# The output gate of a gated recurrence: four projection jobs become two pairs of seven block products

## The chip, the core and the metric

The kernel runs on one core of a Trainium2 chip. Its engines run side by side and wait for each other through semaphores: TensorE (PE in the profile, with its weight loads as PEld) multiplies matrices into PSUM; VectorE (DVE), ScalarE (ACT) and GpSimd (POOL) work on elements; SyncE (SP), ScalarE and GpSimd issue the transfers between memory and SBUF. The metric is the device time of one execution in microseconds (us), lower is better.

## What is computed

One hybrid residual block on 1024 tokens of width 1024, in float32. Two branches read the same normalised input; a sigmoid gate for each merges them; an MLP follows. The part around the change, cut from the reference:

```python
u = xn @ w_in[layer]
q_sb, k_sb, v_sb, f_raw, i_hg, q_hg, g_hg, gate_sb, gate_hg = jnp.split(u, list(c), axis=-1)
o_sb = merge_heads(stick_breaking_attention(...))
f = lb + (1.0 - lb) * jax.nn.sigmoid(f_raw)
o_hg = hgrn2_chunkwise(silu(q_hg), (1.0 - lb) * sigmoid(-f_raw), i_hg, log(f))
o_hg = merge_heads(rmsnorm(o_hg, hg_norm_g)) * jax.nn.silu(g_hg)
g_a = jax.nn.sigmoid(gate_sb + bg[:D_MODEL])
g_b = jax.nn.sigmoid(gate_hg + bg[D_MODEL:])
merged = g_a * (o_sb @ w_o_sb) + g_b * (o_hg @ w_o_hg)
h = x + merged @ w_out
```

`g_hg`, the output gate of the recurrent branch, has four heads of 128 columns. `gate_sb` and `gate_hg`, the branch gates, have 1024 columns each.

## The kernel before

**How a product is made.** Every float32 operand is split into a high part (a cast to fp32r, on ScalarE) and a low part (the difference, on VectorE); `hi_lo` issues both. A product of two such operands takes three matmuls (`three`): high by high, high by low, low by high. One matmul is 128 x 128 weights by 512 tokens, so a projection of the 1024 tokens to 128 columns takes 8 chunks x 2 token halves x 3 = 48 matmuls.

**Two streams on TensorE.** The matmuls of the attention and of the recurrence are the "main" lane. Between them the program sets steps of a stream of other jobs, `st` ("fill"), mostly six matmuls a step. The job order is the order of `st.add`. `st.advance(n, upto)` lets the stream run n steps but not past job `upto`; `st.finish(upto)` runs all up to it. When a job starts, `Stream.prefetch` splits the weights of the next one and loads those of the one after it. TensorE's instruction order is thus written out in program order.

**Stages.** Attention; then the recurrence, head by head: `hg_levels(h)` (decay products on VectorE, scores on TensorE, named sl, at seven levels) side by side with `hg_tail(h - 1)` (state sums pkv, outputs pho, norm, transposes pot). At each step of either, `FILL[h]` steps of the stream are added. Then the gate stage `gates()`, then the output projection and the MLP.

**Block products.** The branch gates are made as products of 2 x 2 blocks in seven multiplications in place of eight: two token halves and two input halves by two column blocks, gate_sb's and gate_hg's columns of one block `cb`. For each of eight `cb`, `raw_job(cb)` runs three plain products in the recurrence: bank pga takes two, pgq the third (on a weight sum, `split_t`), 36 matmuls. The partial sums go to memory (`pd`), the first finished gate too (`gd`). The other four products are on sums of input halves, the "forms" of `sum_forms()`, in the gate stage: `GatePair.x6`, `y5`, `x7`, `y3`, 12 matmuls each into banks gX and gY. For `sum_forms` the low parts of the input are made whole again in place by accumulating transfers from GpSimd's queue (`whole_input`, L1343, tiles xnl). Form sums gs1, gs2 and so on follow on VectorE. `sum_forms` is stepped by the matmul steps of the sb projection.

**The sb projection.** `sb_job(cp)`, four jobs of 96 matmuls (two column blocks `cb`, banks pys), multiplies the attention output with w_o_sb and the first gate.

**Buffers.** Split weights live in the pool `wpool`, two buffers for each tag: `whi` and `wlo` for the parts, `raw` for what was loaded. The units of the stream, the sb weights (wo00 to wo03) and the weights of a gate pair (`whig`, `wlog`: products 6 and 3) use the same two. The weights of products 5 and 7 (`tgh`, `tgl`) are in wide slots.

**The output gate before.** `hg_jobs(h)` adds three plain projections for each head: f, q and g (names pjf, pjq, pjg). `silu_epilogue` leaves silu(g) in a slot. At the end of `hg_tail` VectorE multiplies transposed output, norm weight and gate in one instruction, and `a_hg.put` splits the result for w_o_hg's product (pyh, in the gate stage).

Of the kernel before, what the change touches and what calls it, by code (L numbers as in the profile page):

```python
# [13 lines left out]
AF = mybir.ActivationFunctionType  # L14
ALU = mybir.AluOpType
# [4 lines left out]
P = 128  # L20
# [19 lines left out]
def kernel(  # L40
# [387 lines left out]
    class Unit:  # L428


        late = False
        roomy = ()

        def split_t(self):
# [45 lines left out]
    class Stream:  # L480
# [18 lines left out]
        def prefetch(self):  # L499
            nxt = []  # L500
            for us, _ in self.jobs[self.pos + 1 :]:
                nxt += [u for u in us if u.hl is None]
                if len(nxt) >= 2:
                    break
            if nxt:
                nxt[0].split()
                nxt[0].split_t()
            if len(nxt) > 1:
                nxt[1].load()

# [422 lines left out]

        return ep

    j_hg, j_q = {}, {}

    def hg_jobs(h):
        for key, c0, ep in (
            ("f", C_F, f_epilogue(h)),  # L940
            ("q", C_QH, silu_epilogue(h, "q")),
            ("g", C_GH, silu_epilogue(h, "g")),
        ):
            u = cols_unit(f"w{key}{h}", [(W_IN, c0 + h * P, P)])
            j_hg[h] = proj_jobs([(f"pj{key}{h}", u, ep)], xn)
            if key == "q":
                j_q[h] = j_hg[h]

    hg_jobs(0)

    ones = cpool.tile([P, P], F32R, tag="ones", name="ones")
    nc.gpsimd.memset(ones.bitcast(F32), 1.0)
# [163 lines left out]
            yield  # L1116

    def hg_tail(h):
        dec, k, q, g, v, sc = (hg.pop((h, n)) for n in ("pp", "k", "q", "g", "v", "sc"))
        fc = small.tile([P, NT], F32, tag="fc", name=f"fc{h}")  # L1120
        nc.vector.tensor_copy(fc, chunks(dec)[:, :, P - 1])
        kh, qh, ktk, Ss = k, q, dec, k
# [52 lines left out]
        for half, cs in halves():  # L1175
            open_block("main")
            pot = bank(f"pot{h}_{half}")
            for j in range(4):
                js = slice(j * P, (j + 1) * P)
                transpose(pot[:, js], ons[half][:, js])  # L1180
            nc.vector.scalar_tensor_tensor(
                out=g[:, cs],
                in0=pot,
                scalar=prm[:, HGN + h : HGN + h + 1],
                in1=g[:, cs],
                op0=ALU.mult,
                op1=ALU.mult,
            )
            yield
        ohg[h] = g  # L1190


    class Split:
# [27 lines left out]

    pd = [dram(f"pd{cb}", [P, 2, 512]) for cb in range(KT)]
    gd = [dram(f"gd{cb}", [P, 512]) for cb in range(KT)]
    yd = [dram(f"yd{cb}", [P, 2, 512]) for cb in range(KT)]


# [21 lines left out]
        return prm[:, BG + which * KT + cb : BG + which * KT + cb + 1]  # L1250

    def gate_cols(which, cb):
        c0 = (C_GA, C_GB)[which] + cb * P
        return slice(c0, c0 + P)

    class RawUnit(Unit):
# [27 lines left out]
                self.hl.append((t[:, 0:512], t[:, 512:]))  # L1284
                hi_lo(*self.hl[1], self.raw[1][:, 512:])

    raw_units = [RawUnit(cb) for cb in range(KT)]

    def raw_job(cb):
        u = raw_units[cb]  # L1290

        def steps_of(ps, wt, w0, half_, k0, start):
            wh, wl = u.hl[wt]
            for k in range(4):
                c = (w0 + k) * P
                xh, xl = xn.mov(k0 + k, half_)
                three(
                    ps, wh[:, c : c + P], wl[:, c : c + P], xh, xl, start and k == 0, k == 3, True
                )
                if k % 2 == 1:  # L1300
                    yield

        def body():
            p1, p14, g1 = (half(f"{n}_{cb}") for n in ("p1", "p14", "g1"))
            ps, p4 = bank(f"pga{cb}"), bank(f"pgq{cb}")
            if cb >= 6:
                load_g1(cb - 6)
            if 3 <= cb < KT - 1:
                osb[cb - 3] = slot(f"osr{cb}")
                load(osb[cb - 3], od[cb - 3])  # L1310
            yield from steps_of(ps, 0, 0, 0, 0, True)
            hi_behind[0] = nc.scalar.copy(p1, ps)
            nc.scalar.dma_start(pd[cb][:, 0, :], p1)
            if cb == 0:
                u.split_t()
            st.prefetch()
            hi_behind[0] = None
            yield from steps_of(p4, 1, 0, 1, 4, True)
            add(p14, p1, p4)
            if cb == 3 or cb == KT - 1:  # L1320
                whole_input(1, int(cb == KT - 1))
            nc.gpsimd.dma_start(pd[cb][:, 1, :], p14)
            yield from steps_of(ps, 0, 4, 0, 4, False)
            nc.scalar.activation(g1, ps, AF.Sigmoid, bias=gate_bias(0, cb))
            (nc.gpsimd if cb < 2 else nc.scalar).dma_start(gd[cb], g1)
            if cb >= 4:
                a_sb.put(cb - 4, osb.pop(cb - 4))

        return st.add([u], body)
# [16 lines left out]
    def sum_forms():  # L1346


        raw = whole
        def split(m, kp, src):  # L1350
            forms[m, kp] = tuple(slot(f"gs{n}{m}{kp}", F32R) for n in "hl")
            hi_lo(*forms[m, kp], src)

        for j in range(2):
            whole_input(0, j)
        yield from range(WAIT)
        s1, s2 = {}, {}
        for kp in range(2):
            s1[kp], s2[kp] = slot(f"gs1{kp}"), slot(f"gs2{kp}")
            ins = add(s1[kp], raw[1, 0, kp], raw[1, 1, kp])  # L1360
            if kp == 0:
                after(ins, hg_sum[0])
            yield
            sub(s2[kp], s1[kp], raw[0, 0, kp])
            yield
            split(6, kp, s2[kp])
            yield
        for kp in range(2):
            split(5, kp, s1[kp])
            yield  # L1370
        for kp in range(2):
            s3 = slot(f"gs3{kp}")
            sub(s3, raw[0, 0, kp], raw[1, 0, kp])
            yield
            split(7, kp, s3)
            yield
        gp[0].load()
        gp[0].load_sums()
        for kp in range(2):
            s4 = slot(f"gs4{kp}")  # L1380
            sub(s4, raw[0, 1, kp], s2[kp])
            yield
            split(3, kp, s4)
            yield
        yield from range(4)
        gp[0].split()

    def sb_job(cp):
        src = W_OSB[:, cp * 256 : (cp + 1) * 256].rearrange("(k p) c -> p k c", p=P)
# [25 lines left out]
        return st.add([unit], body)  # L1415


    j_raw = []
    hg_jobs(1)
    j_i = i_job()  # L1420
    j_raw.append(raw_job(0))
    hg_jobs(2)
    j_raw.append(raw_job(1))
    j_raw.append(raw_job(2))
    hg_jobs(3)
    j_raw += [raw_job(cb) for cb in range(len(j_raw), KT)]
    j_sb = [sb_job(cp) for cp in range(4)]

    class GatePair:
# [3 lines left out]
        def load(self):  # L1433
# [4 lines left out]
            for i, s_, which in ((0, 0, 0), (0, 1, 1), (1, 1, 1)):  # L1438
# [3 lines left out]
                        "(k p) c -> p k c", p=P  # L1442
                    ),
                )
            self.wo = half(f"wor{cb}")
            load(
                self.wo.rearrange("p (k c) -> p k c", k=4),
# [2 lines left out]

        def load_sums(self):
            cb = self.cb
            self.p, self.y = slot(f"pr{cb}"), slot(f"yr{cb}")
            for t, d in ((self.p, pd), (self.y, yd)):
                load(t.rearrange("p (k t) -> p k t", k=2), d[cb])

        def split(self, behind=None):
            cb = self.cb
# [11 lines left out]
            h, l = (slot(f"tg{n}{cb}", F32R) for n in "hl")  # L1470
            after(hi_lo(h, l, r0), behind)
            self.w.update({5: (h[:, s0], l[:, s0]), 7: (h[:, s1], l[:, s1])})
            h, l = (half(f"wo{n}{cb}", F32R) for n in "hl")
            hi_lo(h, l, self.wo)
            self.hg = h, l
# [15 lines left out]
            return ps  # L1491

        def gate(self, t, which):
            nc.scalar.activation(t, t, AF.Sigmoid, bias=gate_bias(which, self.cb))

        def x6(self):
            self.X = bank(f"gX{self.cb}")
# [17 lines left out]
            self.gate(p14, 0)  # L1515

        def late_half(self):
            ps = self.hg_product(1)
            p1, p14, y = self.p[:, 0:512], self.p[:, 512:1024], self.y[:, 512:1024]
            mul(y, y, p14)  # L1520
            mul(p1, p1, ps)
            add(y, y, p1)
            self.out(1, y)
# [4 lines left out]
            self.gate(self.u2, 1)  # L1528

        def early_half(self):  # L1530
            ps = self.hg_product(0)
            y = self.y[:, 0:512]
            mul(self.u2, self.u2, ps)
# [37 lines left out]
            return lo  # L1571

    last_form, owed_lo = {}, []
    gp = [GatePair(cb) for cb in range(KT)]
    gates_in = [gp[4 * i + j] for j in range(4) for i in range(2)]

    def gates():
        for v, n, m in zip(gates_in, gates_in[1:] + [None], gates_in[2:] + [None] * 2):
# [7 lines left out]
            else:  # L1586
                out_form["11"].split(1)
                last_lo[0] = v.u2_sum
                out_form["11"].split()
            v.x7()  # L1590
            v.late_half()
            v.y3()
            v.early_half()
        owed_lo.pop()()


# [600 lines left out]
    scores(*items[1])  # L2197
    st.finish(j_qk[0])

    n_fill = 9 * (j_q[1] - j_qk[0]) + 9  # L2200
    n_first = 3
    ready = deque()
    wsums = out_weight_sums()
# [1 line left out]
    for i, it in enumerate(items):  # L2205
# [5 lines left out]
        if i % 2 == 1:  # L2211
            next(wsums, None)
        want = n_first + (i + 1) * (n_fill - n_first) // len(items)
        st.advance(want - done, j_q[1])
        done = want
        before = ready.popleft() if ready else None

# [8 lines left out]
            between()  # L2226
        if r:
            ready.append(r)
    st.finish(j_q[1])
    st.advance(1, j_hg[1])  # L2230
    while ready:
        values(*ready.popleft())


    FILL = (3.75, 3.3, 2.7, 2.5, 2.9)
    owed = 0.0
    for h in range(NHG + 1):
        lev = hg_levels(h) if h < NHG else iter(())
        tail = hg_tail(h - 1) if h > 0 else iter(())
        upto = (j_hg[2], j_hg[3], j_raw[5], j_sb[1], j_sb[3])[h]  # L2240
        going = True
        while going:
            going = False
# [4 lines left out]
                    st.advance(int(owed), upto)  # L2248
                    owed -= int(owed)
        if h + 1 < NHG:  # L2250
            st.finish(j_hg[h + 1])
        if h > 1:
            a_hg.put(h - 2, ohg[h - 2], hg_level[0])
    a_hg.put(NHG - 1, ohg[NHG - 1])
    st.finish(j_sb[3])
    gates_in[1].load()
    gates()

# [97 lines left out]
```

## Time and profile before

| What | Value |
|---|---|
| Median of three runs | 1442.32 us (1441.84 to 1443.24) |
| The profiled execution: its time / its span | 1442.05 / 1440.2 us |
| Mean granted TensorE clock | 0.999 |
| Head 0 of the recurrence, about | 307 to 342 us |
| Head 3, about | 508 to 559 us |
| Gate stage | 609 to 740 us |

In a row of groups, out<-in names the tiles, then partitions x elements, a count, busy time and mean ns of one, and the idle time of the engine before them with what ended it. A row of a wait list has the total, the count and the longest wait in us. A row of the chain has start, length and what ran. A row of a timeline has start, length, engine and line, tiles, and the idle time before it in brackets.

### The profile page before, as it was taken

The numbers are of one execution on the slowest core, as the hardware profiler recorded it, in microseconds if no ns is written. First come the engines' busy times: TensorE is split into PE (matmuls) and PEld (weight loads), VectorE is DVE, ScalarE is ACT, GpSimd is POOL, SyncE is SP. The second block draws the span as 40 slices with busy tenths as digits, with TensorE's granted clock in tenths as the row PEclk, the third lists the DMA queues.
The fourth block names the chain that finished last, engine by engine and source line by source line (L and its number), as shares of the span: only waits on it lengthen the run. The fifth ranks groups of instructions, "written<-read, shape, count | busy, mean of one in ns | idle before, by whom it ended". The sixth has DMA issues, their size and how long they took to land.

```text
span 1440.2 us, 19612 instructions
## 1 busy us (share of the span) xinstructions
PE 1430.0 (99%) x7272; PEld 1210.0 (84%) x7272; DVE 1106.4 (77%) x1583; ACT 665.7 (46%) x1151; POOL 137.8 (10%) x338
## 2 busy tenths in 40 slices
PE   9999999999999999999999999999999999999998
PEld 8989988888888888888888888888888888888886
DVE  6799898988467798788787898666666757768765
ACT  7566666652223334433335574444444433523443
POOL 3121132200000012100000300000000000000032
PEclk9999999999999999999999999999999999999999
DMA  7235154332113349745477415344445974776825
GB/s 213 49 94 131 30 110 75 74 81 59 52 45 103 88 161 260 239 166 178 149 287 249 163 43 190 128 142 155 160 147 211 346 267 169 261 275 240 281 99 187
DMA packets 157751, 228.85 MB, mean 159 GB/s; under 512 B 25772, under 2 KB 91864, under 8 KB 157656
## 3 DMA queue, kind: packets, MB, share of 16 engines
q1 hardware_dynamic: 142680, 186.96, 38.4%
q0 software_dynamic: 11520, 34.61, 9.2%
q10 hardware_dynamic: 3456, 6.03, 1.1%
q8 instruction: 57, 0.93, 0.3%
q14 instruction: 38, 0.31, 0.1%
HBM read 164.12 MB, written 63.44 MB: 158 GB/s over the span
## 4 chain that ended last, share of the span: by engine, by line
PE 95%; DVE 2%; DMA 1%; issue 1%; POOL 1%; ACT 1%; SPq 0%; DVEq 0%; POOLq 0%; ACTq 0%
PE pm L128 21%; PE pX L128 9%; PE pW L128 6%; PE pY L128 6%; PE pjqk L128 6%; PE pga L128 3%; PE pjq L128 3%; PE pjf L128 3%; PE pys L128 3%; PE pyh L128 3%; PE gY L128 3%; PE gX L128 3%; PE po L128 3%; PE z L128 2%; PE pjv L128 2%; PE pjg L128 2%
## 5 line engine op out<-in xcount | busy, mean ns | idle before, releaser
L151 ACT CAST whid<-w 128x1024 fp32r<-128x1024 f32 x30 | 31.6, 1054 | 153.3 <-PE pm L128 88.7
L784 DVE TENSOR_TENSOR_SCAN rm<-rm,bits 128x511 f32<-128x511 f32 (+7 forms) x72 | 87.3, 1219 | 13.8 <-ACT rm L762 13.6
L128 PE MATMUL pm<-wlod,sh 128*128 128x512 f32 x240 | 93.4, 389 | 0.0
L128 PE MATMUL pm<-whid,sh 128*128 128x512 f32 x240 | 93.4, 389 | 0.0
L128 PE MATMUL pm<-whid,sl 128*128 128x512 f32 x240 | 93.4, 389 | 0.0
L128 PE MATMUL pm<-tl,sh 128*128 128x512 f32 (+1 forms) x210 | 81.3, 387 | 0.0
L128 PE MATMUL pm<-th,sl 128*128 128x512 f32 (+1 forms) x210 | 81.3, 387 | 0.0
L128 PE MATMUL pm<-th,sh 128*128 128x512 f32 (+1 forms) x210 | 81.3, 387 | 0.0
L156 DVE TENSOR_TENSOR wlod<-w,whid 128x1024 fp32r<-128x1024 f32 x30 | 36.7, 1223 | 54.6 <-ACT whid L151 54.4
L156 DVE TENSOR_TENSOR sl<-sa,sh 128x1024 fp32r<-128x1024 f32 x56 | 68.2, 1218 | 1.0 <-ACT sh L151 1.0
L151 ACT CAST wTh<-pw 128x512 fp32r<-128x512 f32 (+2 forms) x96 | 43.9, 486 | 51.5 <-PE pw L131 51.0
L151 ACT CAST sh<-sa 128x1024 fp32r<-128x1024 f32 x56 | 57.2, 1046 | 8.2 <-DMA sa<-ad 8.2
L1995 POOL TENSOR_SCALAR fss<-fss 128x1 f32<-128x1 f32 x8 | 4.4, 552 | 562.1 <-ACT fsc L1990 561.6
L156 DVE TENSOR_TENSOR wTl<-pw,wTh 128x512 fp32r<-128x512 f32 (+2 forms) x96 | 50.6, 548 | 3.9 <-ACT wTh L151 3.2
L128 PEld LDWEIGHTS pm<-wlod,sh 128*128 128x128 f32 x240 | 45.1, 188 | 9.4
L128 PEld LDWEIGHTS pm<-whid,sh 128*128 128x128 f32 x240 | 45.0, 188 | 9.4
L128 PEld LDWEIGHTS pm<-whid,sl 128*128 128x128 f32 x240 | 45.1, 188 | 9.3
L164 DVE TENSOR_TENSOR bt<-bt,rm 128x511 f32<-128x511 f32 (+7 forms) x72 | 48.9, 685 | 3.8
L128 PE MATMUL pX<-sql,t1h 128*128 128x512 f32 x128 | 50.0, 391 | 0.1
L128 PE MATMUL pX<-sqh,t1l 128*128 128x512 f32 x128 | 49.8, 389 | 0.0
L128 PE MATMUL pX<-sqh,t1h 128*128 128x512 f32 x128 | 49.8, 389 | 0.0
L762 ACT ACTIVATE rm<-z 128x511 f32<-128x511 f32 (+4 forms) x96 | 48.0, 501 | 3.0 <-PE z L128 1.2
(921 smaller groups left out, 4518.2 us busy)
## 6 DMA issues: line engine op xcount, KB each, us to landing
w<-in_w_ff_dram SPq DMA_DIRECT2D x72, 512.0 KB, 5.3
sa<-ad SPq DMA_DIRECT2D x56, 512.0 KB, 6.4
ad<-a SPq DMA_DIRECT2D x32, 256.0 KB, 2.1
ad<-s SPq DMA_DIRECT2D x16, 512.0 KB, 5.7
tw<-in_w_out_dram POOLq DMA_DIRECT2D x24, 256.0 KB, 3.8
x<-in_x_dram SPq DMA_DIRECT2D x8, 512.0 KB, 9.1
xnl<-xnh POOLq DMA_DIRECT2D x8, 512.0 KB, 11.2
pr<-pd SPq DMA_DIRECT2D x8, 512.0 KB, 6.1
```

Source lines behind the costliest of these rows:

```text
L128: return pe(nc.tensor.matmul(*a, **k))
L151: hi_last[0] = after(in_turn("act", nc.scalar.copy(dst, src)), hi_behind[0])
L156: nc.vector.tensor_tensor(out=dst, in0=src, in1=hi.bitcast(F32), op=ALU.subtract),
L164: return nc.vector.tensor_tensor(out=out, in0=a, in1=b, op=ALU.mult)
L762: nc.scalar.activation(rm[:, s0 + c0 - 1 : s0 + m - 1], z[:, c0:m], AF.Sigmoid, scale=-0.125)
L784: sc = nc.vector.tensor_tensor_scan(out=rr, data0=rr, data1=bits[:, 1024 - nk + a : 1024 - nk + b][:, ::-1], initial=rm[:, b : b + 1] if i ...
L1995: nc.gpsimd.tensor_scalar(out=ssq, in0=ssq, scalar1=1.0 / D, scalar2=EPS, op0=ALU.mult, op1=ALU.add)
```

## The change

The four jobs of g go away. Two more units `RawUnit` and two more pairs `GatePair` (cb 8 and 9; `NG = KT + 2`) take their place: pair 8 holds the columns of heads 0 and 1, pair 9 those of heads 2 and 3. Their three plain products are in the recurrence, their four products on sums at the head of the gate stage. The recurrence's tail now only scales (on ScalarE); gating and splitting of the four heads (`gated`, with `a_hg.put`) come in the gate stage. The order of jobs, the amounts of fill, and where the last sb job ends are changed with it.

```diff
-    hg_jobs(0)
+    for h in range(2):
+        f_job(h)
+        q_job(h)
+    q_job(2)
...
-            nc.vector.scalar_tensor_tensor(
-                out=g[:, cs],
-                in0=pot,
-                scalar=prm[:, HGN + h : HGN + h + 1],
-                in1=g[:, cs],
-                op0=ALU.mult,
-                op1=ALU.mult,
-            )
+            nc.scalar.activation(
+                on_t[:, cs], pot, AF.Copy, scale=prm[:, HGN + h : HGN + h + 1]
+            )
...
-        c0 = (C_GA, C_GB)[which] + cb * P
+        if cb < KT:
+            c0 = (C_GA, C_GB)[which] + cb * P
+        else:
+            c0 = C_GH + (2 * (cb - KT) + which) * P
...
-            nc.scalar.activation(g1, ps, AF.Sigmoid, bias=gate_bias(0, cb))
-            (nc.gpsimd if cb < 2 else nc.scalar).dma_start(gd[cb], g1)
+            if cb < KT:
+                nc.scalar.activation(g1, ps, AF.Sigmoid, bias=gate_bias(0, cb))
+            else:
+                nc.scalar.activation(g1, ps, AF.Sigmoid)
+                mul(g1, ps, g1)
+            nc.scalar.dma_start(gd[cb], g1)
...
-    hg_jobs(1)
+    f_job(2)
     j_i = i_job()
-    j_raw.append(raw_job(0))
-    hg_jobs(2)
-    j_raw.append(raw_job(1))
-    j_raw.append(raw_job(2))
-    hg_jobs(3)
-    j_raw += [raw_job(cb) for cb in range(len(j_raw), KT)]
+    raw_job(KT)
+    f_job(3)
+    raw_job(KT + 1)
+    q_job(3)
+    j_raw = [raw_job(cb) for cb in range(KT)]
...
+        def gated(self, which, first, second):
+            h = 2 * (self.cb - KT) + which
+            for (_, cs), t in zip(halves(), (first, second)):
+                mul(ohg[h][:, cs], ohg[h][:, cs], t)
+            a_hg.put(h, ohg[h])
...
-    gates_in = [gp[4 * i + j] for j in range(4) for i in range(2)]
+    gates_in = gp[KT:] + [gp[4 * i + j] for j in range(4) for i in range(2)]
+
+    SB_HELD = {KT: 2, KT + 1: 1, 0: 1}
...
+            st.advance(SB_HELD.get(v.cb, 0), j_sb[3])
             v.x7()
             v.late_half()
+            st.advance(SB_HELD.get(v.cb, 0), j_sb[3])
             v.y3()
             v.early_half()
+            if v.cb == 0:
+                st.finish(j_sb[3])
...
-    FILL = (3.75, 3.3, 2.7, 2.5, 2.9)
+    FILL = (3.4, 2.6, 2.3, 2.2, 2.7)
...
-        upto = (j_hg[2], j_hg[3], j_raw[5], j_sb[1], j_sb[3])[h]
+        upto = (j_f[3], j_raw[1], j_raw[5], j_sb[1], j_sb[2])[h]
...
-        if h > 1:
-            a_hg.put(h - 2, ohg[h - 2], hg_level[0])
-    a_hg.put(NHG - 1, ohg[NHG - 1])
-    st.finish(j_sb[3])
+            st.finish(max(j_f[h + 1], j_q[h + 1]))
+    st.finish(j_sb[2])
```

In attention the stream now holds f and q of heads 0 and 1 and q of head 2, where it held f, q and g of head 0 and f and q of head 1. For pairs 8 and 9, `split` and `load` leave the w_o_hg part out and `load_sums` fetches `gd` in place of `yd`. The weight sum of unit 8 is split one step later than the others (`ahead = False`).

More of the change, by code (lines that the diff above doesn't have):

```diff
@@ L431 @@
         late = False
+        ahead = True
         roomy = ()
@@ L506, in prefetch @@
                 nxt[0].split()
-                nxt[0].split_t()
+                if nxt[0].ahead:
+                    nxt[0].split_t()
             if len(nxt) > 1:
@@ L934, in silu_epilogue, with f_job, q_job @@
         return ep
[L936 to L947, printed above, removed]
-    hg_jobs(0)
+    j_f, j_q = {}, {}
+    def f_job(h):
+        u = cols_unit(f"wf{h}", [(W_IN, C_F + h * P, P)])
+        j_f[h] = proj_jobs([(f"pjf{h}", u, f_epilogue(h))], xn)
+    def q_job(h):
+        u = cols_unit(f"wq{h}", [(W_IN, C_QH + h * P, P)])
+        j_q[h] = proj_jobs([(f"pjq{h}", u, silu_epilogue(h, "q"))], xn)
+    for h in range(2):
+        f_job(h)
+        q_job(h)
+    q_job(2)
     ones = cpool.tile([P, P], F32R, tag="ones", name="ones")
@@ L1118, in hg_tail @@
     def hg_tail(h):
-        dec, k, q, g, v, sc = (hg.pop((h, n)) for n in ("pp", "k", "q", "g", "v", "sc"))
+        dec, k, q, v, sc = (hg.pop((h, n)) for n in ("pp", "k", "q", "v", "sc"))
+        on_t = slot(f"on{h}")
         fc = small.tile([P, NT], F32, tag="fc", name=f"fc{h}")
@@ L1180, in hg_tail @@
                 transpose(pot[:, js], ons[half][:, js])
-            nc.vector.scalar_tensor_tensor(
-                out=g[:, cs],
-                in0=pot,
-                scalar=prm[:, HGN + h : HGN + h + 1],
-                in1=g[:, cs],
-                op0=ALU.mult,
-                op1=ALU.mult,
+            nc.scalar.activation(
+                on_t[:, cs], pot, AF.Copy, scale=prm[:, HGN + h : HGN + h + 1]
             )
             yield
-        ohg[h] = g
+        ohg[h] = on_t
     class Split:
@@ L1219, in sub @@
         return nc.vector.tensor_tensor(out=out, in0=a, in1=b, op=ALU.subtract)
-    pd = [dram(f"pd{cb}", [P, 2, 512]) for cb in range(KT)]
-    gd = [dram(f"gd{cb}", [P, 512]) for cb in range(KT)]
+    NG = KT + 2
+    pd = [dram(f"pd{cb}", [P, 2, 512]) for cb in range(NG)]
+    gd = [dram(f"gd{cb}", [P, 512]) for cb in range(NG)]
     yd = [dram(f"yd{cb}", [P, 2, 512]) for cb in range(KT)]
@@ L1285, in split_t @@
                 hi_lo(*self.hl[1], self.raw[1][:, 512:])
-    raw_units = [RawUnit(cb) for cb in range(KT)]
+    raw_units = [RawUnit(cb) for cb in range(NG)]
+    raw_units[KT].ahead = False
     def raw_job(cb):
@@ L1305, in body @@
             ps, p4 = bank(f"pga{cb}"), bank(f"pgq{cb}")
-            if cb >= 6:
+            if 6 <= cb < KT:
                 load_g1(cb - 6)
@@ L1313, in body @@
             nc.scalar.dma_start(pd[cb][:, 0, :], p1)
-            if cb == 0:
-                u.split_t()
+            u.split_t()
             st.prefetch()
@@ L1323, in body @@
             yield from steps_of(ps, 0, 4, 0, 4, False)
-            nc.scalar.activation(g1, ps, AF.Sigmoid, bias=gate_bias(0, cb))
-            (nc.gpsimd if cb < 2 else nc.scalar).dma_start(gd[cb], g1)
-            if cb >= 4:
+            if cb < KT:
[4 more added lines that the diff above has]
+            nc.scalar.dma_start(gd[cb], g1)
+            if 4 <= cb < KT:
                 a_sb.put(cb - 4, osb.pop(cb - 4))
@@ L1376, in sum_forms @@
             yield
-        gp[0].load()
-        gp[0].load_sums()
+        gates_in[0].load()
+        gates_in[0].load_sums()
         for kp in range(2):
@@ L1385, in sum_forms @@
         yield from range(4)
-        gp[0].split()
+        gates_in[0].split()
     def sb_job(cp):
@@ L1415, in sb_job @@
         return st.add([unit], body)
-    j_raw = []
-    hg_jobs(1)
+    f_job(2)
     j_i = i_job()
-    j_raw.append(raw_job(0))
-    hg_jobs(2)
-    j_raw.append(raw_job(1))
-    j_raw.append(raw_job(2))
-    hg_jobs(3)
-    j_raw += [raw_job(cb) for cb in range(len(j_raw), KT)]
+    raw_job(KT)
[3 more added lines that the diff above has]
+    j_raw = [raw_job(cb) for cb in range(KT)]
     j_sb = [sb_job(cp) for cp in range(4)]
@@ L1444, in load @@
                 )
+            if cb >= KT:
+                return
             self.wo = half(f"wor{cb}")
@@ L1452, in load_sums @@
             cb = self.cb
-            self.p, self.y = slot(f"pr{cb}"), slot(f"yr{cb}")
-            for t, d in ((self.p, pd), (self.y, yd)):
-                load(t.rearrange("p (k t) -> p k t", k=2), d[cb])
+            self.p = slot(f"pr{cb}")
+            load(self.p.rearrange("p (k t) -> p k t", k=2), pd[cb])
+            if cb >= KT:
+                load_g1(cb)
+                return
+            self.y = slot(f"yr{cb}")
+            load(self.y.rearrange("p (k t) -> p k t", k=2), yd[cb])
         def split(self, behind=None):
@@ L1472, in split @@
             self.w.update({5: (h[:, s0], l[:, s0]), 7: (h[:, s1], l[:, s1])})
+            if cb >= KT:
+                return
             h, l = (half(f"wo{n}{cb}", F32R) for n in "hl")
@@ L1493, in gate @@
         def gate(self, t, which):
-            nc.scalar.activation(t, t, AF.Sigmoid, bias=gate_bias(which, self.cb))
+            if self.cb < KT:
+                nc.scalar.activation(t, t, AF.Sigmoid, bias=gate_bias(which, self.cb))
+            else:
+                s = half(f"gs{self.cb}")
+                nc.scalar.activation(s, t, AF.Sigmoid)
+                mul(t, t, s)
+        def gated(self, which, first, second):
[3 more added lines that the diff above has]
+            a_hg.put(h, ohg[h])
         def x6(self):
@@ L1517, in late_half @@
         def late_half(self):
+            if self.cb >= KT:
+                self.gated(0, g1r[self.cb], self.p[:, 512:1024])
+                return
             ps = self.hg_product(1)
@@ L1530, in early_half @@
         def early_half(self):
+            if self.cb >= KT:
+                self.gated(1, self.u2, self.p[:, 0:512])
+                return
             ps = self.hg_product(0)
@@ L1573 @@
     last_form, owed_lo = {}, []
-    gp = [GatePair(cb) for cb in range(KT)]
-    gates_in = [gp[4 * i + j] for j in range(4) for i in range(2)]
+    gp = [GatePair(cb) for cb in range(NG)]
+    gates_in = gp[KT:] + [gp[4 * i + j] for j in range(4) for i in range(2)]
+    SB_HELD = {KT: 2, KT + 1: 1, 0: 1}
     def gates():
@@ L2198 @@
     st.finish(j_qk[0])
-    n_fill = 9 * (j_q[1] - j_qk[0]) + 9
+    n_fill = 9 * (j_q[2] - j_qk[0]) + 9
     n_first = 3
@@ L2213 @@
         want = n_first + (i + 1) * (n_fill - n_first) // len(items)
-        st.advance(want - done, j_q[1])
+        st.advance(want - done, j_q[2])
         done = want
@@ L2228 @@
             ready.append(r)
-    st.finish(j_q[1])
-    st.advance(1, j_hg[1])
+    st.finish(j_q[2])
+    st.advance(1, j_f[2])
     while ready:
         values(*ready.popleft())
-    FILL = (3.75, 3.3, 2.7, 2.5, 2.9)
+    FILL = (3.4, 2.6, 2.3, 2.2, 2.7)
     owed = 0.0
@@ L2250 @@
         if h + 1 < NHG:
-            st.finish(j_hg[h + 1])
-        if h > 1:
-            a_hg.put(h - 2, ohg[h - 2], hg_level[0])
-    a_hg.put(NHG - 1, ohg[NHG - 1])
-    st.finish(j_sb[3])
+            st.finish(max(j_f[h + 1], j_q[h + 1]))
+    st.finish(j_sb[2])
+    for _ in side[0]:
+        pass
     gates_in[1].load()
```

## The prediction

> **What bounds the kernel now.** I read the page's first part, then what TensorE waits for, then the chain of work that ended last.
>
> ```profile
> span 1440.2 us, 19612 instructions
> PE 1430.0 (99%) x7272; PEld 1210.0 (84%) x7272; DVE 1106.4 (77%) x1583; ACT 665.7 (46%) x1151; POOL 137.8 (10%) x338
> ...
> PE warm L128 <- POOL ident masks.py:199: 2.2, 1, 2.2
> PE pjqk L128 <- DVE xnl L334: 0.3, 1, 0.3
> PE po L128 <- ACT wTh L151: 0.2, 1, 0.2
> PE pjv L128 <- ACT wv0h L151: 0.2, 1, 0.2
> PE sl L128 <- DVE q L164: 0.2, 1, 0.2
> ```
>
> The wait list is short: about 3 us in 1440, most of it before the first matmul. So TensorE's own stream sets the end: a matmul removed is worth its whole slot, and every wait that the change puts into that stream is paid in full, for no idle time lies around to take it up. The chain gives the price of a slot, and what TensorE does from the last gate product of the recurrence into the gate stage:
>
> ```profile
> 551.73 2.94 PE pgq L128 x12
> 554.67 0.61 PE sl L128 x8
> ...
> 555.97 2.97 PE pga L128 x12
> 558.94 0.77 PE pk L131 x7
> 559.70 2.75 PE pys L128 x12
> 562.45 1.56 PE pkv L128 x14
> ...
> 583.37 25.87 PE pys L128 x114
> 609.24 2.72 PE gX L128 x12
> 611.96 2.72 PE gY L128 x12
> ```
>
> Twelve 128x512 matmuls in an unbroken stretch take 2.72 us, 0.227 us each (25.87 / 114 gives the same). A group's mean is something else:
>
> ```profile
> L128 PE MATMUL pjg<-xnh,wg3h 128*128 128x512 f32 x16 | 6.5, 409 | 0.0
> ```
>
> This is the view of groups by shape: 409 ns is how long one matmul is in flight while its neighbours overlap it. The saving is counted at 0.227.
>
> **The matmuls saved.** Before, the output gate is four jobs pjg of 48 matmuls, 192. After, it is two more block-product pairs, 8 and 9 (two heads each): 24 on pga and 12 on pgq in the recurrence, 24 on gX and 24 on gY in the gate stage, 84 each, 168. Everything else on TensorE keeps its count. 24 fewer x 0.2267 = **-5.44 us**.
>
> **Engine work that moves.** The eight fused multiplies of hg_tail become eight copies with a scale on ScalarE; eight gating multiplies, the hi cast and lo subtraction of the four heads, and the weight sums and splits of two more pairs go to the gate stage. What may hide them, by stretches of the span:
>
> ```profile
> 508.40:559.00 50.60, 50.59 (x311) 43.10 (x311) 47.39 (x92) 20.51 (x42) 9.80 (x14) 1.00 0.65 203
> 559.00:609.20 50.20, 50.20 (x252) 42.40 (x251) 40.02 (x48) 22.76 (x42) 8.59 (x13) 1.00 0.82 245
> 609.20:625.50 16.30, 16.30 (x74) 13.49 (x73) 11.73 (x17) 5.80 (x8) 0.00 (x0) 1.00 0.68 227
> 625.50:739.80 114.30, 114.30 (x506) 94.66 (x505) 89.88 (x129) 37.21 (x50) 9.20 (x17) 1.00 0.52 170
> ```
>
> Columns: stretch, length, busy PE, PEld, DVE, ACT, POOL, clock, DMA share. Head 3 (first row) has VectorE at 94%, the gate stage (last two) at 78%, so in bulk the move is hidden: 0. Three dependences are not.
>
> **Term 1: the two-deep ring of gate weights.** The tags whi and wlo have two buffers. Before, the last weight of the sb projection (wo03) dies with its last pys product and whig0 has been cast long before; the chain goes from pys to gX with no gap. After, the job of wo03 is held open through pairs 8, 9 and 0 (SB_HELD), so one of the two buffers stays taken, and each next pair needs the other one, which the previous pair's product 3 (gY) reads to its end. In the built order, whig9's cast waits for the last but one matmul of gY8, and TensorE goes straight from gY8 to gX9; whig0 stands so to gY9 and gX0, and whig8 to the last pys of block 5, before gX8. The price is one cast and one subtraction in series:
>
> ```profile
> L151 ACT CAST whig<-wg4r 128x1024 fp32r<-128x1024 f32 x1 | 1.1, 1052 | 3.6 <-DVE wg4r L1219 3.6
> L156 DVE TENSOR_TENSOR wlog<-wg4r,whig 128x1024 fp32r<-128x1024 f32 x1 | 1.2, 1224 | 0.0
> ```
>
> 1.05 + 1.22 = 2.28 us from the release until the third matmul of gX (the first that reads wlog) may go; it is covered by the ring's one outstanding matmul and gX's first two, some 2 slots or 0.45: **1.84 each** for pairs 9 and 0. For pair 8 VectorE stands in line with more in front (two form subtractions, a form sum and two halves' multiplies just before wlog8): a further 0.9, 2.75. Sum **+6.4**; at least 3 x 1.84 = 5.5, at most 3 x 2.75 = 8.3. From pair 4 on the ring is free again and nothing changes.
>
> **Term 2: a wait for a transfer in head 3.** The form sums read the halves of the input, whose low parts GpSimd's queue turns whole again by accumulating transfers (rows of GpSimd's and VectorE's timelines, and of the transfers' landing times):
>
> ```profile
> 495.49 0.95 POOL L1343 DMA_DIRECT2D xnl<-xnh  x1 [21.07 <-PE pjg L128]
> ...
> 553.38 0.86 POOL L1343 DMA_DIRECT2D xnl<-xnh  x1 [1.83 <-PE pgq L128]
> ...
> xnl<-xnh POOLq DMA_DIRECT2D x1, 512.0 KB, 11.4
> ...
> DMA to landing us min/median/max: 4.7/11.2/16.9
> ...
> 563.71 2.33 DVE L1147 SCALAR_TENSOR_TENSOR k<-k,fc,pkv 128x128 f32<-128x128 f32 x6
> 565.95 1.22 DVE L1216 TENSOR_TENSOR gs<-xnl,xnl 128x1024 f32<-128x1024 f32 x1
> 567.21 1.23 DVE L1219 TENSOR_TENSOR gs<-gs,xnl 128x1024 f32<-128x1024 f32 x1
> ```
>
> The transfer issued at 553.38 needs 11.4 us, so its data (xnl12) are there at 564.8, 10.1 us behind the end of pgq7 (554.67). Before, the first form sum comes behind the state sums of head 3 (563.71) and finds them landed. After, one job less is left for head 3, the sb projection starts earlier in it, and the built order of VectorE has gs10 and gs20 directly behind p14_7 and **in front of the k and q products of level 5**, which TensorE's next scores (sl3_6) read. TensorE reaches sl3_6 after pot2_1 (4 small, 0.44), the second half of pga7 (2.72), sl3_5 (1.2) and 12 pys (2.72), 7.1 us behind pgq7. VectorE releases it at 10.1 + 1.22 + 1.23 + two products, each:
>
> ```profile
> 556.98 0.41 DVE L164 TENSOR_TENSOR k<-k,pp 128x256 f32<-128x256 f32 x1
> 557.32 0.41 DVE L164 TENSOR_TENSOR q<-q,pp 128x256 f32<-128x256 f32 x1
> ```
>
> that is 13.3: **+6.2 us**. Behind sl3_6 nothing else comes late (the next pys weights and k have 2.72 us of matmuls to get ready). Bounds from the landing: with the least row, 4.7, sl3_6 finds its data and this is 0; with the greatest, 16.9, it is 11.7. I take 11.4, the row of the same transfer with the same ones queued around it.
>
> [...]
>
> **Term 3: less fill in head 0.** FILL falls from 3.75 to 3.4 steps of six matmuls per recurrence step, 0.35 x 6 x 0.227 = 0.48 us less cover each time, while VectorE's chain there is as long as it was:
>
> ```profile
> 325.77 1.22 DVE L156 TENSOR_TENSOR sl_l<-sl_x,sl_h 128x1024 fp32r<-128x1024 f32 x1
> ...
> 327.67 0.39 PE L128 MATMUL sl<-sl_l,ones 128*128 128x512 f32 x1
> ...
> 341.90 2.05 PE L128 MATMUL sl<-q,k 128*128 128x128 f32 x16 [0.16 <-DVE q L164]
> ```
>
> sl_l is ready at 326.99 and read 0.7 us later; three recurrence steps in, 1.4 us of cover are gone, some of it met by work of VectorE that has left this stretch. I take 0.5 there and 0.2 at two later levels, **+0.9**, between 0 and 2 (0.16 is the wait that the last row has already). Heads 1 and 2 keep spare time on VectorE; the attention and everything behind the merge keep their order: 0.
>
> **Sum.** -5.44 + 6.4 + 6.2 + 0.9 = +8.1 on the profiled execution's 1442.05 us (its span is 1440.2), 1450.1; the median of the runs is 0.27 above that execution, so 1450.4.
>
> **Rivals.**
>
> A. *The saving is kept whole*: 1442.3 - 5.4 = 1436.9, faster. It needs the casts of gate weights to run ahead as they did before and gs10 to find its data. For it: a wait list of 3 us, by which the kernel was in balance with just such casts. Against: whi has two buffers and both have readers when gY8 runs. 7%.
>
> B. *The transfer lands early*: eight transfers of the kind took 4.7 to 16.9 us, and the two that were issued with little beside them landed soonest; if the traffic around pgq7 is thinner now, term 2 goes and -5.44 + 6.4 + 0.9 = +1.9 is left, 1444.2. Against: the same six transfers come in the same few microseconds. 15%.
>
> C. *The transfer lands later still*: GpSimd's queue carries two more stored products, ScalarE's the stored gates that left it, and the sb weights are read in the same stretch. At the row's 16.9 term 2 is 11.7, 1455.9. It decides from a landing of 13 us on. 15%.
>
> D. *The clock falls in the long wait.* TensorE never stands longer than 2.2 us in the trace, so no row shows what 6 us of idleness do to the granted clock (1.00 in all four stretches above). Were it halved there and for the next twelve matmuls, these would take 2.72 us more, 1453.1. 8%. [...]
>
> That the change doesn't do what it says is excluded by the matmul counts.
>
> **How the numbers follow.** The forecast, both stalls, has 55%: 1450.4. Noise between runs is about 0.2% (2.9 us). Faster by more: A, 7%. Within it: B, 15%. Slower: the forecast, C and D, 78%. The range reaches down to B's lower part, -5.44 + 5.5 + 0 + 0.9 = +1.0, 1443.3, a little below it for what runs vary, 1442.5, and up to C's, 1456; A lies outside.
>
> **What would show it.** TensorE's wait list: sl waiting for DVE q by about 6 us once, in head 3, with VectorE's gs<-xnl,xnl released by a DMA just before; gX waiting three times for whig and wlog, 1.8 to 2.8 us in all each. If the first is missing, B was right; if the second, the ring was not the limit and A's side is. A granted clock under 1.00 just behind the sl wait would be D. If pyh of pair 0 waits for ahgl, the gating chain that I hid was not hidden, and the forecast is wrong upward. No matmul row may differ in its slot: twelve at 2.72 us.

## The result, and the profile after

The changed kernel takes 1451.92 us (median of 6 runs, 1450.68 to 1454.34) where the kernel before takes 1442.03 (6 runs). The ratio is 1.0070, 95% interval 1.0057 to 1.0083: slower by 0.7%, 1.5 us above the forecast.

The page of the changed kernel, and its list of what TensorE waited for (total, count, longest, us):

```profile
span 1449.2 us, 19649 instructions
PE 1427.9 (99%) x7248; PEld 1204.8 (83%) x7248; DVE 1122.7 (77%) x1609; ACT 674.3 (47%) x1165; POOL 142.0 (10%) x338
...
PE gX L128 <- ACT whig L151: 3.0, 3, 1.1
PE sl L128 <- DVE pp L164: 2.7, 1, 2.7
PE warm L128 <- POOL ident masks.py:199: 2.2, 1, 2.2
PE gX L128 <- DVE wlog L156: 1.8, 3, 0.7
PE pgq L128 <- ACT wga8t L151: 1.2, 1, 1.2
PE gX L128 <- DVE gu L1214: 1.1, 1, 1.1
PE sl L128 <- DVE sl_l L156: 0.8, 2, 0.4
...
PE sl L128 <- DVE q L164: 0.3, 1, 0.3
```

TensorE executed 24 matmuls fewer (7272 to 7248), as the counts said. Its waits rose from about 3 us to 14: the saving was more than given back, for the most part in waits that this list names one by one. The first and fourth rows are term 1 of the prediction and the second is term 2; the fifth and sixth are new.

Term 1 in the chain that ended last, from pair 8 into 9 and from 9 into 0 (start, length, what ran):

```profile
593.46 2.51 PE gY L128 x11
595.97 0.02 issue
595.99 1.05 ACT whig L151
...
597.07 1.24 DVE wlog L156
...
598.35 2.57 PE gX L128 x10
600.92 2.72 PE gY L128 x12
...
609.08 2.51 PE gY L128 x11
...
611.65 1.05 ACT whig L151
...
612.73 1.24 DVE wlog L156
...
613.98 3.29 DMA wg4r<-in_w_in_dram
...
618.05 0.60 DVE on L164
...
621.06 0.61 DVE gu L1214
```

The cast starts when the eleventh matmul of gY has gone and the subtraction follows it; two matmuls of gX run beside the pair, so the chain shows ten of gX behind it. Before, the chain went from pys to gX and on with nothing between. From 595.97, with one matmul of gY and twelve of gX to go, to 600.92 are 4.95 us; 13 slots of 0.227 are 2.95: 2.0 are lost. For pair 8 TensorE's timeline shows it matmul by matmul (start, length in flight, idle time before):

```profile
577.04 0.39 PE L128 MATMUL pys<-asbh,wo02l 128*128 128x512 f32 x1
578.55 0.50 PE L128 MATMUL gX<-gsh,whig 128*128 128x512 f32 x1 [1.12 <-ACT whig L151]
578.89 0.39 PE L128 MATMUL gX<-gsl,whig 128*128 128x512 f32 x1
580.00 0.50 PE L128 MATMUL gX<-gsh,wlog 128*128 128x512 f32 x1 [0.72 <-DVE wlog L156]
580.34 0.40 PE L128 MATMUL gX<-gsh,whig 128*128 128x512 f32 x1
```

577.04 to 580.34 is 3.30 us for four slots (0.91): 2.4 lost, where the wait list counts 1.8. Each of these two waits costs about 0.3 us more than its row says: the idle time of the first counts only from the end of the matmul in flight (577.43), and each time the first matmul behind the wait holds its slot for 0.34 (578.55 to 578.89, 580.00 to 580.34), not 0.23.

Term 2, VectorE's and TensorE's timelines in head 3, and the landing of the transfer issued at 526.74:

```profile
530.43 0.68 DVE L1214 TENSOR_TENSOR p<-p,pgq 128x512 f32<-128x512 f32 x1
534.68 1.23 DVE L1214 TENSOR_TENSOR gs<-xnl,xnl 128x1024 f32<-128x1024 f32 x1 [3.57 <-DMA xnl<-xnh]
535.94 1.23 DVE L1217 TENSOR_TENSOR gs<-gs,xnl 128x1024 f32<-128x1024 f32 x1
537.08 0.41 DVE L164 TENSOR_TENSOR k<-k,pp 128x256 f32<-128x256 f32 x1
...
537.98 1.94 PE L128 MATMUL sl<-q,k 128*64 128x64 f32 x16 [2.70 <-DVE pp L164]
539.85 0.80 PE L128 MATMUL pys<-asbh,wo00h 128*128 128x512 f32 x1
540.45 0.63 PE L128 MATMUL pys<-asbl,wo00h 128*128 128x512 f32 x1
...
xnl<-xnh POOLq DMA_DIRECT2D x1, 512.0 KB, 7.9
```

VectorE stands 3.57 us for the transfer with level 5's products (the row of k, and of q and pp behind it) still to come, and TensorE stands 2.70 us for those. What follows is a second cost of the same wait. Stretches of the span (length, busy PE, PEld, DVE, ACT, POOL, granted clock, DMA share, GB/s):

```profile
520.00:535.00 15.00, 15.00 (x106) 12.49 (x104) 11.43 (x24) 7.89 (x12) 6.44 (x8) 1.00 0.98 244
535.00:537.60 2.60, 0.28 (x2) 0.00 (x0) 2.56 (x4) 0.40 (x1) 0.00 (x0) 1.00 1.03 264
537.70:541.00 3.30, 3.02 (x19) 2.74 (x20) 3.30 (x8) 1.12 (x2) 0.00 (x0) 0.50 1.09 271
```

The granted clock is 0.50 in the last row's 3.3 us, from just before the end of the wait (537.98) on: the two pys rows above start 0.60 us apart, where a slot in an unbroken stretch at a clock of 1.00 is 0.227.

From pwW, where the output projection begins, to the end the kernels hardly differ (700.7 and 700.4 us): nearly all of the loss lies ahead.

### The profile page after: what moved, and what is told of

Read it like the earlier page. It is cut to its first block, busy times and chain, and to the rows that moved or that the text cites. A ratio compares the mean times of both kernels' runs of the same rounds, so it can differ in the third digit from the quotient of the medians.

```text
span 1449.2 us, 19649 instructions
## 1 busy us (share of the span) xinstructions
PE 1427.9 (99%) x7248; PEld 1204.8 (83%) x7248; DVE 1122.7 (77%) x1609; ACT 674.3 (47%) x1165; POOL 142.0 (10%) x338
## 4 chain that ended last, share of the span: by engine, by line
PE 90%; DVE 4%; DMA 2%; issue 1%; ACT 1%; POOL 1%; SPq 0%; POOLq 0%; DVEq 0%; ACTq 0%
PE pm L128 21%; PE pX L128 9%; PE pW L128 6%; PE pY L128 6%; PE pjqk L128 6%; PE gX L128 4%; PE gY L128 4%; PE pjq L128 3%; PE pjf L128 3%; PE pyh L128 3%; PE po L128 3%; PE pji L128 2%; PE z L128 2%; PE pjv L128 2%; PE pwX L128 2%; PE pys L128 2%
## 5 line engine op out<-in xcount | busy, mean ns | idle before, releaser
L164 DVE TENSOR_TENSOR bt<-bt,rm 128x511 f32<-128x511 f32 (+7 forms) x72 | 48.9, 685 | 3.9
```

The lines of the kernel that those rows point to most:

```text
L164: return nc.vector.tensor_tensor(out=out, in0=a, in1=b, op=ALU.mult)
```

## The experiments

Eight kernels ran, each a variation of the changed kernel. Times are medians; the kernel before, run beside them, took 1441.69 us in the first four and 1441.81 in all.

**e1_level: the form sum kept behind the level products.**

```diff
-                after(ins, hg_sum[0])
+                after(after(ins, hg_sum[0]), hg_level[0])
```

> The changed kernel, with the first form sum gs10 kept behind the level products of head 3 issued so far. Theory (the form sums wait for the transfer in front of products that TensorE needs, and the long wait halves the clock): the 2.7 us wait of sl goes, the granted clock stays at 1.00 in head 3, which gives back 1.7 more: 1451.9 - 4.4 = 1447.5. Rival (VectorE is simply full in head 3): the wait comes back at pk, pkv or the next pys, and the time stays above 1450.5.

1448.37 us (1.0045, interval 1.0033 to 1.0058). The wait of sl for pp is gone, and so is the low clock:

```profile
520.00:545.00 25.00, 25.00 (x167) 20.90 (x166) 21.67 (x45) 11.12 (x17) 7.01 (x9) 1.00 0.97 240
```

TensorE is busy throughout, at full clock, in a stretch that before the edit held the wait. Nothing waits at pk, pkv or pys in its place. Between the first pys and pk both kernels run the same matmuls; first the changed kernel's rows:

```profile
532.27 0.50 PE L128 MATMUL pys<-asbh,wo00h 128*128 128x512 f32 x1
...
543.27 0.93 PE L131 MATMUL pk<-ident,k 128*128 128x128 f32 x7
```

and e1_level's:

```profile
534.05 0.50 PE L128 MATMUL pys<-asbh,wo00h 128*128 128x512 f32 x1
...
540.92 0.93 PE L131 MATMUL pk<-ident,k 128*128 128x128 f32 x7
```

11.0 us against 6.9: the wait for the transfer costs 4.1, of which 2.7 is idle time and 1.4 the low clock and the restart. 3.6 us came back on the medians, 0.9 less than expected; the list of waits has a new one of 0.9 at the start of head 3 (sl for ACT sl_h). It stands ahead of the edited instructions, here and in e2_wide, which has 0.9 of it too; e6_fill, e7_early and e8_all have 0.2 to 0.5, and the changed kernel and the other three have none. No run tests what makes it come and go.

**e2_wide: the last sb weights out of the ring.**

```diff
-        unit = Unit(f"wo0{cp}", [[(0, 256, src)]])
+        unit = Unit(f"wo0{cp}", [[(0, 256, src)]], wide=cp == 3)
```

> The changed kernel, with the weights of the last sb job in wide slots instead of the two-deep ring. Theory (the ring of whi and wlo sets the three waits before gX): the waits of pairs 9 and 0 go (1.8 us each), that of pair 8 (2.2) shrinks to what VectorE's queue leaves of it, about 1: 1451.9 - 4.7 = 1447.2. Rival (VectorE's or the loads' lateness sets them): gX waits as long, only for another tile, and the time stays above 1450.5.

1448.39 us (1.0043, 1.0031 to 1.0056): 3.5 us came back of the expected 4.7, with the 0.9 for sl_h standing against them. From its wait list, and one of ScalarE's casts:

```profile
PE sl L128 <- DVE pp L164: 2.7, 1, 2.7
PE gX L128 <- DVE wlog L156: 1.1, 1, 1.1
PE gX L128 <- DVE gu L1214: 0.5, 1, 0.5
PE gX L128 <- ACT whig L151: 0.2, 1, 0.2
...
588.86 1.06 ACT L151 CAST whig<-wg9r 128x1024 fp32r<-128x1024 f32 x1 [7.70 <-DVE wg9r L1217]
```

Of the six waits of gX for whig and wlog, the four of pairs 9 and 0 are gone, since whig9 is now cast when its weights are there and not when gY8 ends. Pair 8 keeps 0.2 + 1.1. The wait for gu, for which nothing was edited, fell from 1.1 to 0.5: a load of pair 4 stands behind wlog0 in the chain above, and VectorE's work behind that load, so part of the ring's lateness had been handed on. The wait of 2.7 in head 3 stays.

**e3_both: the two together.**

> Both edits, the form sum kept back and the last sb weights in wide slots. If the two costs are independent, their gains add: 1451.9 - 4.4 - 4.7 = 1442.8, level with the kernel before. If one takes the other's place, it stays near the better of the two, 1447.

1442.62 us (1.0005, 0.9996 to 1.0014): within 0.2 us of the expected sum, and the loss against the kernel before is gone. Neither edit takes the other's place. The 9.3 us are 2.2 more than the 7.1 that the two gave alone (3.6 and 3.5); the wait for sl_h, which stood in each of those two and is not here, goes some way to fill the gap. What its list still holds:

```profile
PE pgq L128 <- ACT wga8t L151: 1.2, 1, 1.2
PE gX L128 <- DVE wlog L156: 1.1, 1, 1.1
PE sl L128 <- DVE sl_l L156: 0.9, 2, 0.5
PE gX L128 <- DVE gu L1214: 0.5, 1, 0.5
```

**e4_nothold: the last sb job finished ahead of the gate stage**, which undoes one part of the change.

```diff
-    SB_HELD = {KT: 2, KT + 1: 1, 0: 1}
+    SB_HELD = {}
...
-    st.finish(j_sb[2])
+    st.finish(j_sb[3])
```

> The changed kernel, with the last sb job finished ahead of the gate stage instead of held open through pairs 8, 9 and 0. Theory of the ring: whig9 and whig0 find a free buffer, 3.6 us of waits go; but 42 matmuls, 9.5 us, of cover for the gating of the four heads go too, and pyh of pair 0 waits for ahgl by some 3 to 5 us: 1451.9 - 3.6 + 4 = 1452.3, with the waits at another place. Rival (the ring isn't the cause): gX of pairs 9 and 0 waits for whig as before.

1447.79 us (1.0042, 1.0029 to 1.0054). The waits for whig and wlog are gone, and others have come, as expected of the ring:

```profile
PE sl L128 <- DVE pp L164: 2.9, 1, 2.9
PE gX L128 <- DVE gu L1214: 2.3, 2, 1.3
...
PE gY L128 <- DVE pr L1214: 1.1, 1, 1.1
```

The expected time was missed: it was 1452.3. Place and amount both differ. TensorE waits for pr and gu, sums which VectorE reads out of the banks that the next product writes, and not for the split gates ahgl; the cover that the held job gives is worth 2.3 us here (3.4 of waits of this kind, against 1.1), not 3 to 5. Holding the job open thus cost more in the ring than it hid.

**e5_split, e6_fill, e7_early: three groups of small waits, one at a time**, each on e3_both. wga8t is split at the head of its job; head 0 has its old fill; pair 8's weights are split four steps sooner.

```diff
+            if cb == KT:
+                u.split_t()
             yield from steps_of(ps, 0, 0, 0, 0, True)
...
-    FILL = (3.4, 2.6, 2.3, 2.2, 2.7)
+    FILL = (3.75, 2.6, 2.3, 2.2, 2.7)
...
-        yield from range(4)
         gates_in[0].split()
```

> The kernel of e3_both, and the weight sum of unit 8 (wga8t) split at the head of its job instead of just before the product that reads it. Theory: the wait of pgq for wga8t (1.4 us longer than a slot) is the cost of that split standing behind the copy of pga's first half; it goes: 1442.6 - 1.4 = 1441.2. Rival: ScalarE or VectorE is late there anyway, and sl of head 1 waits in its place: 1442.6.

> The kernel of e3_both, with the fill of head 0 back at 3.75 steps. Theory of term 3: the waits of sl in head 0 (0.5, 0.5 and 0.4 us over a slot) fall to what the kernel before had there (0.5 together): 1442.6 - 0.9 = 1441.7. Rival: fill spent in head 0 is missing behind it, and head 0's end waits instead: 1442.6.

> The kernel of e3_both, with pair 8's weights split four fill steps earlier. Theory: what is left of pair 8's wait (whig 0.3, wlog 1.2 us over a slot) is VectorE's queue in front of the split, and falls to 0.3: 1442.6 - 1.2 = 1441.4. Rival: the loads of wg8 arrive late, and the wait stays: 1442.6.

1441.21, 1441.34 and 1441.36 us, each 1.3 to 1.4 below e3_both's 1442.62. In e5_split the wait of pgq has left the list. In e6_fill that of sl for q has left it, and so has that for sl_l in head 0 (0.4; the one of 0.5 in head 3 is left), but 0.5 for sl_h has come at the start of head 3, and the list as a whole is no shorter. In e7_early the waits for whig and gu have left, and wlog keeps 0.7 where 0.3 was expected; VectorE still has a form subtraction, two weight sums and a split in front of it. Single runs of one of these kernels lie up to 3.6 us apart. That each edit takes away the waits it was aimed at is shown by the lists; the sizes of the three gains are known only to about a microsecond.

**e8_all: all five edits.**

> All of it: form sum kept back, last sb weights in slots, wga8t split at the job's head, fill of head 0 at 3.75, pair 8 split earlier. If the costs add, 1442.6 - 1.4 - 0.9 - 1.2 = 1439.1, which is 0.2% below the kernel before: of the 5.4 us of saved matmuls 2.5 to 3 would then be left. If the waits feed each other, 1441 to 1442.

1438.09 us (1.0 below the expected sum); ratio 0.9973, interval 0.9962 to 0.9983. It beats the changed kernel and the kernel before. Its page and list:

```profile
span 1437.5 us, 19648 instructions
...
PE gX L128 <- DVE wlog L156: 0.7, 1, 0.7
PE sl L128 <- DVE sl_l L156: 0.6, 1, 0.6
PE xnt L131 <- DVE x L624: 0.5, 1, 0.5
PE sl L128 <- ACT sl_h L151: 0.3, 1, 0.3
```

Of the 5.4 us of matmuls, 3.7 now reach the end on the medians (1441.8 to 1438.1), and 2.7 on the two profiled executions, whose spans are 1440.2 and 1437.5.

## Why the prediction was right, point by point

**The saving, -5.44 us.** Right in mechanism and, as far as the runs go, in size: 24 matmuls are gone, and a block of twelve still takes 2.72 us. In e8_all the profiled execution stands 2.7 us below the one before, with some 2 us of waits in its list that the other did not have (wlog, sl_l, sl_h and xnt, less what was there before). If each of these four waits costs 0.3 more than its row, as the two of pair 8 did, they come to some 3, and 2.7 and 3 make 5.7, near the 5.44.

**Term 1, the ring, +6.4.** Right in place, cause, order and size. Pair 9 lost 2.0, pair 0 as much by its rows in the list, which are alike (1.84 each forecast), and pair 8 2.4 (2.75 forecast): 6.4 to 6.5. e2_wide shows the cause by taking away the buffer's other reader, e4_nothold by taking away the held job.

**Term 2, the transfer in head 3, +6.2.** Right in cause, mis-sized: 4.1 measured, in two parts that partly make up for each other. The transfer landed 7.9 us after its issue (11.4 assumed, from the row of before). With 7.9 the term's own working gives 6.2 - 3.5 = 2.7, and TensorE stood 2.7. And the clock fell, to 0.50, which is rival D's case: the prediction gave it 8%, and only behind a wait of 6 us; that the two errors bring the term nearer to its forecast is luck.

**Term 3, head 0, +0.9.** The list has waits of 0.3 or 0.4 (half of its row for sl_l) and 0.3 there, where before had 0.2; with 0.3, as at pair 8, for the wait that is new, that makes 0.8. In e6_fill, with the old fill, both have left the list. Right, as far as that can be told.

**Two waits were not in the sum.** pgq of unit 8 stands 1.2 us for wga8t, which is split one step later than its fellows: the change above says so, and the prediction put no price on it. e5_split, which splits it sooner, takes the wait away. In the gate stage gX stands 1.1 for gu. Half of that follows from the ring (e2_wide leaves 0.5). The other half goes when pair 8's weights are split sooner (e7_early), which points to VectorE being late: in the chain of the changed kernel VectorE goes through the moved gating multiplies (618.05 on, tiles on, pr, gu, at L164) until just before the sum at 621.06 that releases gX. This is the work that the prediction hid in bulk under a share of 78%. The step that failed is there: the share of the stage was read in place of the chain. That these multiplies alone make the sum late is argued from the chain, and no run tests it. With 0.4 for sl_l in head 3 and, as at pair 8, 0.3 a wait more than the list counts, these are an estimated 3.6 us, against 2.1 by which term 2 came out smaller. The sum so mended is -5.4 + 6.5 + 4.1 + 0.8 + 3.6 = +9.6; the span grew by 9.0. That the forecast came within 1.5 us of the result is thus in part luck: what was left out and what was too large nearly cancel.

**The rivals.** A's two conditions, casts that run ahead and a first form sum that finds its data, are what e2_wide and e1_level made; with both, e3_both took 1442.6 and not 1436.9, for the smaller waits were left, and with the other three edits it is 1438.1. B and C, the landing: 7.9 us lies between B's and the forecast's, and the six runs of the changed kernel, 1450.7 to 1454.3, lie between B's 1444.2 and C's 1455.9. D's clock came true (0.50), at a wait of 2.70 us in place of 6 and a cost of about 1.4 us, where it had 2.7.

## What to carry to other kernels

When an engine has no idle time, count a removed instruction by its slot in an unbroken stretch (0.227 us here) and then look at every resource that the moved work holds longer: here a two-deep ring of weights, one buffer of which a third user held, cost more than the 24 matmuls saved (6.4 against 5.4 us). An instruction that waits for a transfer belongs behind those in its queue that the bounding engine needs next; here the built order had it in front, and e1_level, with it behind, is 3.6 us faster. A share of 78% says nothing of a chain of dependences inside the stage: price each wait at its place.

## What the runs showed of the hardware

In the profiled execution of the changed kernel TensorE's granted clock was halved at a wait of 2.70 us. Its clock records show 0.50 for 3.41 us, from 537.64 us of the span on, and nowhere else until the last matmul is done; the wait for wga8t (1.25 us, at 384) and those before gX (up to 1.12, at 577 to 622) leave it at 1.00. In e1_level, where the 2.70 us wait is gone, it is 1.00 from 520 to 545 us, and in the kernel before, without such a wait, 1.00 from the first record to the last matmul. Behind the last matmul it fell to 0.50 in both kernels' profiled executions: 4.1 us after that matmul's end in the kernel before (1433.23 to 1437.28), 3.4 us after it in the changed kernel (1442.22 to 1445.59).

In the traces of these two kernels the stretches at full clock, from the first record on, are whole multiples of 3.413 us, the length of the stretch at 0.50 in head 3 (1430.18 us are 419 of them in the kernel before; 532.48 are 156 and 904.53 are 265 in the changed one), so there the clock changed on a grid. In the 3.41 us before it fell in head 3, TensorE had stood still for about 2.4 (535.28 to 537.64). How much is needed, and whether it matters where on the grid a wait lies, no run shows. Nor need every execution of a kernel be alike: the mean granted clock of the changed kernel's six runs goes from 0.999 in the shortest (1450.68 us) to 0.995 in the longest (1454.34 us), so the 1.4 us are those of one execution.

The accumulating transfer of 512 KB that decides term 2 took 7.9 us in the changed kernel and 11.4 before, with the same five others around it and the transfer engines at a share of 1.07 while it ran, in both. So in these two the share does not tell how long the transfer takes; what made it shorter after the change, no run tests.
